# Four of 22 feed-forward input groups by Strassen's scheme, their weight differences formed by GpSimd

## The chip, the cores and the metric

The kernel runs on one core of a Trainium2 chip. The core has a matrix engine (TensorE, PE in the profile; its weight loads are shown apart as PEld), VectorE (DVE), ScalarE (ACT), GpSimd (POOL) and SyncE (SP), which here only issues DMAs. The metric is device time of one launch in microseconds, median of the runs.

## The reference

A decoder trunk on 256 tokens of width 2048, in float32. Layer 0 is a recurrent block, layer 1 is windowed attention with sinks, and each is followed by a feed-forward block of hidden width 5632. The feed-forward block is what the change touches:

```python
D_MODEL = 2048
SEQ = 256
D_FF = ((8 * D_MODEL // 3 + 255) // 256) * 256
...
def swiglu_ffn(x, g, w_in, w_out):
    h = rms_norm(x, g)
    gate, up = jnp.split(h @ w_in, 2, axis=-1)
    return x + (jax.nn.silu(gate) * up) @ w_out
...
for layer in range(DEPTH):
    ...
    x = swiglu_ffn(x, norm2_g[layer], ffn_w_in[layer], ffn_w_out[layer])
```

## The kernel before, in words

**Layout.** Activations are kept transposed: features on the 128 partitions, 256 tokens (T) along the columns, so x is 16 tiles of 128x256. Each float32 operand is split into a high part in the format fp32r and the rest, a low part of the same format; a product is three matmuls, high by high, high by low, low by high.

**Jobs.** All weight matrices are cut into jobs of 512 KB: 256 rows (two tiles of 128) by 512 columns, on the chip 128x1024. Every job goes the same way, in `stream` (L278): SyncE loads it into one of four `raw` buffers (`load`, four jobs ahead); ScalarE copies it to one of four `hi` buffers, which rounds it (L264), and VectorE subtracts, raw - hi, into one of four `lo` buffers (L267), three jobs ahead; then its matmuls run. A `hi` and `lo` pair comes free when TensorE has done the job four before; a `raw` buffer, when its split is done.

**Groups.** `group` (L347) runs the jobs of 512 output columns over the whole inner dimension, 8 jobs for an inner dimension of 2048: 4 column tiles by 2 row tiles by 3 products, 24 matmuls of 256 columns a job, weights loaded into the array and activations streaming. Sums stay in PSUM. Of four PSUM banks two are used whole ("two"): there the high weight may multiply the high and low part of the activations in one matmul of 512 columns. `products` (L296) puts three such matmuls in a row at set places (`SYNC`) and behind any other work of TensorE (`pe_other`, L334). A group with `paired` holds its four sums in two banks and has no 512-column matmuls.

**Feed-forward input.** 22 groups a layer. The columns of a group are gate, up, gate, up for two hidden tiles. At a group's end `done` brings the four sums from PSUM, scales them by the norm (`rstd`), and a background task does silu(gate) * up and splits it into a hidden tile. The norm's factor comes late, from `norm` (L466): TensorE sums the squares, and VectorE and ScalarE form the reciprocal root.

**Order.** The instructions are recorded job by job. Between them `run_bg` lets background tasks (evacuations, norms, gains, softmax) add instructions as long as estimates of VectorE's and ScalarE's time stay under limits. Each engine works its own queue in this order. Intermediate tiles are 58 numbered slots of 128x512 and 8 halves, reused first in, first out.

**GpSimd** does nothing before but the element-wise work of attention (L940, L942, L984).

## Time and profile before

| | |
|---|---|
| median of 3 runs | 1980.52 us (1980.26 to 1980.54) |
| profiled execution, first to last instruction | 1978.9 us |
| TensorE matmuls / weight loads busy | 1971.8 / 1930.5 us |
| VectorE / ScalarE / GpSimd busy | 1256.3 / 1063.0 / 70.5 us |
| HBM read | 371.88 MB, 189 GB/s over the span |
| granted TensorE clock | 1.00 in every stretch asked for |

In the groups of instructions a row gives line, engine, operation, output<-inputs by the program's names without their numbers, shape and count; then the busy time in us and the mean of one in ns; then the engine's idle time ahead of them and what ended it. In a timeline a row gives start, duration (of a row of equal instructions, from the first start to the last end), and in brackets the idle time just before. Records on one engine overlap a little, so the time that an instruction takes in a row is from start to start. A row of stretches gives for each engine the busy us and the number of instructions, then the clock, the share of the DMA engines and GB/s.

### The profile page before, as it was taken

Reading aid. Unit: us, or ns where it says so; the run is one execution under the profiler, and the core shown is the slowest. Engines: PE = TensorE matmul, PEld = TensorE weight load, DVE = VectorE, ACT = ScalarE, POOL = GpSimd, SP = SyncE. Lnnn points to the kernel's source line nnn. Section 1 sums busy time; section 2 is a strip of 40 time slices with the busy share of each in tenths; the row PEclk is TensorE's granted clock in tenths of the full one; section 3 lists DMA queues with packets and bytes.
Section 4 is the critical chain, followed back from the end, with each engine's and each line's share of the span. In section 5 each row is a group of like instructions: output and inputs, shape, how many; then the busy total and the mean of one; then the engine's idle time right before and its main releaser. Section 6 shows DMA issues by size and latency. Waiting matters only on the chain.

```text
span 1978.9 us, 40162 instructions
## 1 busy us (share of the span) xinstructions
PE 1971.8 (100%) x16683; PEld 1930.5 (98%) x16683; DVE 1256.3 (63%) x1981; ACT 1063.0 (54%) x1606; POOL 70.5 (4%) x100
## 2 busy tenths in 40 slices
PE   9999999999999999999999999999999999999999
PEld 9999999999999999999999889999999999999999
DVE  8988876556556655545668776755655565554443
ACT  7798655444444444434556775544544454443342
POOL 0000000000000000000002461000000000000000
PEclk9999999999999999999999999999999999999999
DMA  8555655655556555555655335555565556666663
GB/s 289 185 180 189 212 190 190 197 194 192 192 194 195 196 192 193 192 195 196 195 183 180 130 128 168 190 196 192 192 193 196 196 190 196 193 195 204 208 205 126
DMA packets 106198, 377.10 MB, mean 191 GB/s; under 512 B 11936, under 2 KB 14368, under 8 KB 106016
## 3 DMA queue, kind: packets, MB, share of 16 engines
q1 hardware_dynamic: 105408, 373.88, 57.7%
q8 instruction: 130, 2.13, 0.4%
q10 hardware_dynamic: 608, 0.66, 0.1%
q14 instruction: 52, 0.43, 0.1%
HBM read 371.88 MB, written 2.10 MB: 189 GB/s over the span
## 4 chain that ended last, share of the span: by engine, by line
PE 97%; ACT 1%; DVE 1%; issue 0%; POOL 0%; DMA 0%; ACTq 0%; POOLq 0%
PE b L330 93%; PE b L341 1%; PE b L664 1%; ACT s L116 1%; PE b L338 1%; PE b L850 1%; DVE lo L267 0%; ACT hi L264 0%; DVE s L918 0%; PE b L859 0%; PE b L860 0%; PE b L861 0%; DMA x<-in_x 0%; DVE s L125 0%; DVE s L129 0%
## 5 line engine op out<-in xcount | busy, mean ns | idle before, releaser
L330 PE MATMUL b<-s,hi 128*128 128x256 f32 (+1 forms) x10329 | 1432.1, 284 | 1.1 <-DVE h L125 0.6
L330 PEld LDWEIGHTS b<-s,hi 128*128 128x128 f32 x10329 | 1316.8, 188 | 30.5 <-ACT s L116 1.2
L267 DVE TENSOR_TENSOR lo<-raw,hi 128x1024 fp32r<-128x1024 f32 (+1 forms) x707 | 861.5, 1220 | 655.0 <-ACT hi L264 652.6
L264 ACT ACTIVATE hi<-raw 128x1024 fp32r<-128x1024 f32 (+1 forms) x707 | 746.1, 1056 | 808.6 <-PE b L330 750.7
L330 PE MATMUL b<-s,lo 128*128 128x256 f32 x5504 | 827.9, 276 | 0.0
L330 PEld LDWEIGHTS b<-s,lo 128*128 128x128 f32 x5504 | 718.3, 188 | 0.6
L940 POOL TENSOR_TENSOR s<-s 128x128 f32<-128x128 f32 x32 | 14.8, 463 | 1100.4 <-ACT s L116 1097.6
L116 ACT ACTIVATE s<-h 128x256 fp32r<-128x256 f32 (+1 forms) x106 | 40.7, 411 | 23.5 <-DVE h L125 23.5
L116 ACT ACTIVATE t<-b 128x256 f32<-128x256 f32 x130 | 47.9, 375 | 4.1 <-PE b L330 1.7
L116 ACT ACTIVATE s<-x,par 128x256 fp32r<-128x256 f32 x80 | 38.9, 499 | 20.4 <-DVE x L125 13.7
L116 ACT ACTIVATE s<-s 128x256 f32<-128x256 f32 (+2 forms) x116 | 41.7, 412 | 10.9 <-DVE s L129 7.5
L116 ACT ACTIVATE h<-h 128x256 f32<-128x256 f32 (+1 forms) x104 | 38.9, 376 | 3.7 <-DVE h L125 1.5
L116 ACT ACT_TABLE_LOAD x30 | 38.5, 1283 | 0.6
L129 DVE SCALAR_TENSOR_TENSOR s<-x,par,s 128x256 fp32r<-128x256 f32 x80 | 37.6, 479 | 1.8 <-ACT s L116 1.2
L125 DVE TENSOR_TENSOR x<-x,b 128x256 f32<-128x256 f32 x64 | 24.1, 415 | 21.2 <-PE b L330 21.2
L125 DVE TENSOR_TENSOR h<-b,rstd 128x256 f32<-128x256 f32 x100 | 37.5, 414 | 0.0
L125 DVE TENSOR_TENSOR h<-h,rstd 128x256 f32<-128x256 f32 x94 | 35.3, 416 | 0.0
L125 DVE TENSOR_TENSOR s<-s,s 128x256 fp32r<-128x256 f32 (+2 forms) x84 | 32.4, 416 | 4.1 <-ACT s L116 4.0
L125 DVE TENSOR_TENSOR h<-h,h 128x256 f32<-128x256 f32 x88 | 34.7, 415 | 0.5 <-ACT h L116 0.5
L125 DVE TENSOR_TENSOR s<-h,s 128x256 fp32r<-128x256 f32 x88 | 34.9, 417 | 0.1
L125 DVE TENSOR_TENSOR h<-b,t 128x256 f32<-128x256 f32 x92 | 34.5, 415 | 0.0
L116 ACT ACTIVATE s<-s,h 128x128 f32<-128x128 f32 x64 | 28.2, 442 | 10.2 <-DVE h L134 5.2
(99 smaller groups left out, 612.0 us busy)
## 6 DMA issues: line engine op xcount, KB each, us to landing
raw<-in_ffn_in SPq DMA_DIRECT2D x352, 512.0 KB, 3.4
raw<-in_ffn_out SPq DMA_DIRECT2D x176, 512.0 KB, 3.5
raw<-in_lru_in SPq DMA_DIRECT2D x62, 512.0 KB, 3.8
raw<-in_lru_out SPq DMA_DIRECT2D x32, 512.0 KB, 4.1
raw<-in_w_q SPq DMA_DIRECT2D x32, 512.0 KB, 3.4
raw<-in_w_o SPq DMA_DIRECT2D x32, 512.0 KB, 3.3
raw<-in_gate SPq DMA_DIRECT2D x8, 512.0 KB, 3.7
raw<-in_kv SPq DMA_DIRECT2D x8, 512.0 KB, 4.3
```

The source lines that it names most:

```text
L116: self.nc.scalar.activation(out, in_, func, **kw)
L125: self.nc.vector.tensor_tensor(out, a, b, op)
L129: self.nc.vector.scalar_tensor_tensor(out, a, s, b, op0, op1)
L264: high = self.ins(self.nc.scalar.activation(hi[:, q], raw[:, q], AF.Copy))
L267: self.nc.vector.tensor_tensor(lo[:, q], raw[:, q], hi[:, q].bitcast(F32), ALU.subtract)
L330: self.nc.tensor.matmul(*args, **kw)
L338: self.other = self.ins(f(*args, **kw))
L341: self.other = self.ins(f(*args, **kw))
L664: nc.tensor.matmul(out[j], (hi if high else lo)[:, c:c + P], x2[kt][:, q:q + T], start=kt == 0 and high > q, stop=kt == 1 and not high)
L850: nc.tensor.matmul(ps[f][:, 0:T], w0, x2[kt][:, q:q + T], start=k0 + kt == 0 and high > q, stop=k0 + kt == ND - 1 and not high)
L940: nc.gpsimd.tensor_tensor(o, o, sc[hh][:, 2 * P:3 * P], ALU.add)
```

## The change

In each layer's feed-forward input, groups 0 to 3 are done by Strassen's scheme (Winograd's form, with 7 products for 8). In a Strassen job the 256 rows are two row tiles, the tokens are two halves of 128, and the 512 columns are two halves of 256. So a 2x2 block of activations by a 2x2 block of weights takes 7 products, each three matmuls of 256 columns: 21 a job. Here activations are loaded into the array and the weights stream, and the result has tokens on the partitions.

- **Weights.** The host puts the job's four quarters in another order (`quarters`). Behind each load of such a job GpSimd forms the weight sums (`sums`): two in a slot (t), one in place in the raw buffer, one in a half (t4). `split` then makes high and low parts of raw (1024 columns), t (512) and t4 (256).
- **Activations.** For each pair of tiles `form` makes the four sums of activations: two scaled copies by ScalarE, four GpSimd instructions of 128x128, then a split. It is spawned by `residual` of the projection ahead, and waits for 14 free slots.
- **End of a group.** `fast` combines the four banks (ScalarE once, VectorE four times). Then come the norm's factor per token, silu and product; four transposes on TensorE bring the hidden tiles back to features on partitions. `norm` forms the factor per token too, now for each norm but the first (`if r`): two more sums of one column.
- **Order.** Four jobs of ordinary groups come first, then Strassen jobs and ordinary jobs in turns (32 of each), then the rest. Ordinary groups 4 to 8 have `paired` set to 2: two banks and no 512-column matmuls. The four-bank Strassen group and the two-bank ordinary one leave two banks for the rest.

The core of the diff, without the host's `quarters`, the calls in `run`, and the lines that only hand arguments on:

```diff
+    NS = 4
+    AHEAD = 4
+    SPACE = 14
...
+    def sums(self, i):
+        raw, tt = self.raw[i % 4], self.nc.gpsimd.tensor_tensor
+        b = [raw[:, q * T:(q + 1) * T] for q in range(4)]
+        t, t4 = self.slot(F32), self.half()
+        self.jobs[i][2].update(t=t, t4=t4)
+        t3, t2 = t[:, 0:T], t[:, T:2 * T]
+        tt(t3, b[2], b[0], ALU.subtract)
+        tt(b[0], b[0], b[1], ALU.subtract)
+        tt(t2, b[2], b[0], ALU.subtract)
+        tt(t4, b[3], t2, ALU.subtract)
+
     def split(self, i):
         raw, hi, lo = self.raw[i % 4], self.hi[i % 4], self.lo[i % 4]
+        if len(self.jobs[i]) > 2:
+            s = self.jobs[i][2]
+            t, t4 = s.pop("t"), s.pop("t4")
+            h, l, o = (self.slot() for _ in range(3))
+            s.update(h=h, l=l, o=o)
+            for z, a, b in ((raw, hi, lo), (t, h, l), (t4, o[:, 0:T], o[:, T:2 * T])):
+                self.nc.scalar.activation(a, z, AF.Copy)
+                self.nc.vector.tensor_tensor(b, z, a.bitcast(F32), ALU.subtract)
+            self.free(t)
+            self.free_half(t4)
+            self.dve += 1300
+            self.act += 1200
+            return
...
+    def strassen(self, src, xs, forms, done, last):
...
+                todo = [(0, 0, A(0, 0), B(1)), (1, 1, A(1, 0), B(3)), (1, 0, S(1), t2), (2, 0, S(0), B(0)),
+                        (2, 1, S(2), t3), (3, 0, S(3), B(2)), (3, 1, A(1, 1), t4)]
...
+                    for i, j in ((0, 0), (0, 1), (1, 0)):
+                        self.nc.tensor.matmul(ps[b][:, h * T:h * T + T], w[i], m[j], start=b not in st["begun"],
...
+    def form(self, c, col, out):
+        while len(self.slots) < self.SPACE:
+            yield 1
...
+        tt = self.nc.gpsimd.tensor_tensor
+        tt(s[0], a21, a22, ALU.add)
+        tt(s[2], a11, a21, ALU.subtract)
+        tt(s[1], s[0], a11, ALU.subtract)
+        tt(s[3], a12, s[1], ALU.subtract)
+        yield 3
+        fh, fl = self.slot(), self.slot()
+        self.a(fh, z)
+        self.tt(fl, z, fh.bitcast(F32), ALU.subtract)
...
-        if r == 2:
+        if r:
             n = T + 2
...
+            def fast(ps, g=g):
...
+                self.a(c1, ps[0][:, 0:T])
+                self.tt(two(U[:, :]), two(ps[1][:, :]), twice(c1[:, :]), ALU.add)
+                self.tt(two(V[:, :]), two(ps[2][:, :]), twice(U[:, 0:T]), ALU.add)
+                self.tt(U[:, 0:T], ps[2][:, 0:T], V[:, T:2 * T], ALU.add)
+                self.tt(V, ps[3], V, ALU.add)
...
+            turns += self.strassen(lambda c, g=g: w[g, c], xs, forms, fast, g == self.NS - 1)
+        for g in range(self.NS, NH // 2):
...
-            self.group(lambda c, g=g: w[g, c], ND, xs, done, g == NH // 2 - 1, self.SYNC)
+            self.group(lambda c, g=g: w[g, c], ND, xs, done, g == NH // 2 - 1, self.SYNC,
+                       paired=2 * (g <= 2 * self.NS), jobs=ordinary)
+        n = len(turns)
+        self.jobs += ordinary[:self.AHEAD]
+        for q in zip(turns, ordinary[self.AHEAD:]):
+            self.jobs += q
+        self.jobs += ordinary[self.AHEAD + n:]
```

How the queues change is seen in the order of instructions. VectorE in the first layer's feed-forward input before; lo, raw and hi are the split's buffers, h and s are halves and slots of the hidden tiles:

```order
L267 TENSOR_TENSOR lo_79<-raw_71,hi_75 128x1024
L125 TENSOR_TENSOR s_4346<-h_95,s_4346 128x256
L125 TENSOR_TENSOR s_4360<-h_97,s_4360 128x256
L267 TENSOR_TENSOR lo_80<-raw_72,hi_76 128x1024
L267 TENSOR_TENSOR lo_81<-raw_73,hi_77 128x1024
```

And in the changed kernel, in the turns; line 287 is the split of a Strassen job (raw, t, t4), line 299 that of an ordinary one:

```order
L299 TENSOR_TENSOR lo_82<-raw_74,hi_78 128x1024
L287 TENSOR_TENSOR lo_79<-raw_71,hi_75 128x1024
L287 TENSOR_TENSOR s_4659<-s_4629,s_4658 128x512
L287 TENSOR_TENSOR s_4660<-h_95,s_4660 128x256
L299 TENSOR_TENSOR lo_80<-raw_72,hi_76 128x1024
L287 TENSOR_TENSOR lo_81<-raw_73,hi_77 128x1024
```

Between two splits of 1024 columns there now stand one of 512 and one of 256, in every second job. GpSimd, whose queue is empty at this place before, has four instructions for each Strassen job (lines 273 to 276), two jobs shown:

```order
L273 TENSOR_TENSOR s_4090<-raw_73 128x256
L274 TENSOR_TENSOR raw_73<-raw_73 128x256
L275 TENSOR_TENSOR s_4090<-raw_73 128x256
L276 TENSOR_TENSOR h_100<-raw_73,s_4090 128x256
L273 TENSOR_TENSOR s_4157<-raw_71 128x256
L274 TENSOR_TENSOR raw_71<-raw_71 128x256
```

Each chain works on every second raw buffer. TensorE, at the change from an ordinary job (line 362, weights from hi and lo loaded) to a Strassen job (line 461, hi and lo streaming; names are streaming operand, then loaded one):

```order
L362 MATMUL b_88<-s_3827,hi_78 128x256 x2
L362 MATMUL b_88<-s_3827,lo_82 128x256
L461 MATMUL b_83<-hi_75,s_3470 128x256
L461 MATMUL b_83<-lo_79,s_3470 128x256
L461 MATMUL b_83<-hi_75,s_3470 128x256
L461 MATMUL b_90<-hi_75,s_3484 128x256
```

No 512-column matmul stands in the turns, where before there were three at each place of `SYNC`.

More of the change, by code (lines that the diff above doesn't have):

```diff
@@ new lines, in form @@
+    def form(self, c, col, out):
+        while len(self.slots) < self.SPACE:
+            yield 1
+        g, z = self.slot(F32), self.slot(F32)
+        for h in range(2):
+            k = 2 * c + h
+            self.a(g[:, h * T:h * T + T], self.x[k // 4][:, k % 4, :], scale=self.par[:, col + k:col + k + 1])
+        s = [z[:, n * P:n * P + P] for n in range(4)]
+        a11, a21, a12, a22 = (g[:, n * P:n * P + P] for n in range(4))
+        tt = self.nc.gpsimd.tensor_tensor
[7 more added lines that the diff above has]
+        self.tt(fl, z, fh.bitcast(F32), ALU.subtract)
+        self.free(g)
+        self.free(z)
+        out[c].ap = (fh, fl)
+        out[c].ready = True
+        yield
@@ L427, in gained @@
         xt = self.x[k // 4][:, k % 4, :]
-        for col, vals in gains:
+        for col, vals, *_ in gains:
             g = self.par[:, col + k:col + k + 1]
@@ L503, in residual, with form @@
             return
+        def form(c):
+            for q in gains:
+                if len(q) > 2:
+                    self.spawn(self.form(c, q[0], q[2]))
         def task():
@@ L1089, in run @@
         self.spawn(first())
-        self.lru([(C_N2A, x1)], 1)
-        self.ffn(0, x1, 1, [(C_KVG, xk)], 2)
+        f1, f3 = ([Val() for _ in range(ND // 2)] for _ in range(2))
+        self.lru([(C_N2A, x1, f1)], 1)
+        self.ffn(0, x1, f1, 1, [(C_KVG, xk)], 2)
         self.kv(xk, 2, [(C_N1B, x2)])
-        self.attn(x2, 2, [(C_N2B, x3)], 3)
-        self.ffn(1, x3, 3, None, None, out=d["out"])
+        self.attn(x2, 2, [(C_N2B, x3, f3)], 3)
+        self.ffn(1, x3, f3, 3, None, None, out=d["out"])
         self.stream()
```

89 lines of the change are left out of this document (86 added, 3 removed).

## Prediction

> **What bounds the kernel now.** I read the page's busy times and its chain first.
>
> ```profile
> PE   1971.8 (100%) x16683; PEld 1930.5 (98%) x16683; DVE 1256.3 (63%) x1981; ACT 1063.0 (54%) x1606; POOL 70.5 (4%) x100
> PE 97%; ACT 1%; DVE 1%; issue 0%; POOL 0%; DMA 0%; ACTq 0%; POOLq 0%
> ```
>
> TensorE is on the path for 97% of the span. So fewer matmuls should shorten it, as long as the engines that prepare its operands keep up. How far ahead they are is read from the timeline of a stretch in steady state.
>
> ```profile
> 900.03 1.06 ACT L264 ACTIVATE hi<-raw 128x1024 fp32r<-128x1024 f32 x1 [1.66 <-PE b L330]
> 901.13 1.23 DVE L267 TENSOR_TENSOR lo<-raw,hi 128x1024 fp32r<-128x1024 f32 x1 [1.48 <-ACT hi L264]
> 902.75 1.06 ACT L264 ACTIVATE hi<-raw 128x1024 fp32r<-128x1024 f32 x1 [1.66 <-PE b L330]
> 908.20 1.06 ACT L264 ACTIVATE hi<-raw 128x1024 fp32r<-128x1024 f32 x1 [1.67 <-PE b L330]
> ```
>
> The two engines split one job of weights at a time, and ScalarE starts each split when TensorE gives back a buffer. So the starts of its rows are TensorE's pace: 902.75 - 900.03 = 2.72 us for 24 matmuls of 256 columns, 0.1133 us each. The split that begins at 900.03 is done at 901.13 + 1.23 = 902.36, and its job starts on TensorE three jobs later, at 908.20. VectorE's lead is thus 5.8 us, and it idles 1.48 us a job.
>
> TensorE has a second, slower pace. Behind the sum for a norm (line 338) it stays there for a while:
>
> ```profile
> 306.58 0.59 PE L338 MATMUL b<-acc,con 128*128 128x256 f32 x2
> 307.24 1.10 PE L330 MATMUL b<-s,lo 128*128 128x256 f32 x8
> 326.67 1.23 DVE L267 TENSOR_TENSOR lo<-raw,hi 128x1024 fp32r<-128x1024 f32 x1 [1.60 <-ACT hi L264]
> 329.50 1.23 DVE L267 TENSOR_TENSOR lo<-raw,hi 128x1024 fp32r<-128x1024 f32 x1 [1.60 <-ACT hi L264]
> 900.74 1.07 PE L330 MATMUL b<-s,lo 128*128 128x256 f32 x8
> ```
>
> The same eight matmuls take 1.10 us at 307 and 1.07 us at 900, and a job 329.50 - 326.67 = 2.83 us: 0.118 us for a matmul, 0.0046 more.
>
> **The change, part by part.**
>
> *Matmuls removed.* A Strassen job has 21 matmuls of 256 columns where an ordinary one has 24. Two layers, 4 groups, 8 jobs, 3 each: 192 x 0.1133 = 21.8 us less TensorE work, 10.9 us a layer. The matmuls of 512 columns that vanish from the ordinary groups 4 to 8 are each replaced by two of 256. Those cost no time as such, but they are what the kernel puts behind a disturbance, and between the first and the last Strassen job there are none. So the slower pace can last there. I bound it by all and nothing of 1440 matmuls a layer: 0 to 6.6 us. The K/V projection, which also changes between jobs with weights and jobs with activations as the loaded operand, shows both paces by turns:
>
> ```profile
> 1029.30 0.39 PE L850 MATMUL b<-s,hi 128*128 128x256 f32 x2
> 1031.74 0.40 PE L850 MATMUL b<-s,hi 128*128 128x256 f32 x2
> ```
>
> I take half, 3.3 us a layer.
>
> *TensorE work added.* Four transposes a Strassen group, and two one-column sums (two passes each) in the norm.
>
> ```profile
> 1166.17 0.66 PE L341 MATMUL b<-con,s 128*128 128x128 f32 x4
> 1166.58 0.71 PE L330 MATMUL b<-s,hi 128*128 128x256 f32 x4
> 1025.73 0.50 PE L341 MATMUL b<-con,acc 128*128 128x1 f32 x4
> 1026.09 0.48 PE L850 MATMUL b<-s,hi 128*128 128x256 f32 x2
> ```
>
> From start to the next matmul's start: 0.41 us for four transposes, with the restart about 0.5; and 0.36 us for the columns. That is 4 x 0.5 + 0.4 = 2.4 us a layer. If TensorE stays the bound, a layer gains 10.9 - 3.3 - 2.4 = 5.2 us.
>
> *Work for GpSimd.* Each Strassen job has four TENSOR_TENSOR of 128x256, each operand from SBUF, with line 274 to 276 waiting on the one before. The trace has three groups on that engine:
>
> ```profile
> L942 POOL TENSOR_TENSOR s<-s,h 128x256 f32<-128x256 f32 x32 | 29.9, 955 | 0.2
> L984 POOL TENSOR_TENSOR s<-s,con 128x256 f32<-128x256 f32 x32 | 25.9, 811 | 28.6 <-ACT s L116 27.1
> L940 POOL TENSOR_TENSOR s<-s 128x128 f32<-128x128 f32 x32 | 14.8, 463 | 1100.4 <-ACT s L116 1097.6 <-PE b L341 2.7
> ```
>
> Those means hide two kinds of instruction, and the timelines of GpSimd and VectorE side by side tell them apart:
>
> ```profile
> 1085.12 0.53 DVE L918 CUSTOM_DVE_ANT_0 s<-b,con,par 128x256 f32<-128x256 f32 x1
> 1085.13 0.74 POOL L984 TENSOR_TENSOR s<-s,con 128x256 f32<-128x256 f32 x1
> 1089.66 1.19 POOL L942 TENSOR_TENSOR s<-s,h 128x256 f32<-128x256 f32 x2
> 1191.48 2.17 POOL L942 TENSOR_TENSOR s<-s,h 128x256 f32<-128x256 f32 x2
> 1191.91 1.26 DVE L267 TENSOR_TENSOR lo<-raw,hi 128x1024 fp32r<-128x1024 f32 x1 [0.57 <-ACT hi L264]
> 1193.61 2.42 POOL L984 TENSOR_TENSOR s<-s,con 128x256 f32<-128x256 f32 x2
> 1193.65 1.78 DVE L267 TENSOR_TENSOR lo<-raw,hi 128x1024 fp32r<-128x1024 f32 x1
> ```
>
> Beside a VectorE instruction with one operand in PSUM (line 918) GpSimd's takes 0.74 us and both run undisturbed. Beside a split (line 267, both operands in SBUF) one waits for the other: two of line 942 take 1.19 us at 1089.66 and 2.17 at 1191.48, around a split; and the split at 1193.65, behind a GpSimd instruction that began 0.04 us earlier, takes 1.78 instead of 1.23. So the two never read at once. A GpSimd instruction of 0.74 us takes 0.55 us from a VectorE instruction that waits for it; by the same 0.19 us less, the lighter line 942 (one operand a broadcast column) takes 0.60 - 0.19, about 0.4 to 0.47. The new instructions read two full operands like line 984, so I take 0.55, with 0.45 below and 0.74 above as ends.
>
> The Trainium skill states this as an exclusive lock on a port that VectorE and GpSimd share, held for the whole instruction (page "SBUF — State Buffer", section "SBUF: two separate sides"). That the two exclude each other the trace confirms; the whole instruction it doesn't, since 0.55 us were lost to one of 0.74. By the page's wording the price would be 0.74.
>
> *Work for VectorE.* Its time from start to start, in a row of instructions, is below the recorded mean:
>
> ```profile
> 37.43 3.49 DVE L267 TENSOR_TENSOR lo<-raw,hi 128x1024 fp32r<-128x1024 f32 x3
> 891.72 1.07 DVE L125 TENSOR_TENSOR x<-x,b 128x256 f32<-128x256 f32 x3
> L267 DVE TENSOR_TENSOR lo<-raw,hi 128x512 fp32r<-128x512 f32 x6 | 4.0, 691 | 3.8 <-ACT hi L264 3.7
> ```
>
> (3.49 - 1.23) / 2 = 1.13 us for 1024 columns, (1.07 - 0.41) / 2 = 0.33 for 256, and between them 0.60 for 512 (the row's 0.69 less the same overlap of 0.09). A Strassen job now needs a split of 1024, one of 512 and one of 256.
>
> *The sum on what the two engines share.* Per layer, from the split of the first Strassen job (job 4) to that of the last (job 66), these have both operands in SBUF, counted in the order of instructions: 63 splits of 1024 columns, 71.2 us; 32 of 512, 19.2; 32 of 256, 10.6; 29 others of 256 (products and splits of hidden tiles, the gains, the norm), 9.6; two of 512 for the last activation sums, 1.2. That is 111.8 us of VectorE. GpSimd adds 124 weight differences at 0.55 (those of the first Strassen job are done before), 68.2, and eight instructions of 128 columns at 0.46 - 0.19 = 0.27, 2.2. Together 182.2 us. VectorE has some 16 us more that read PSUM; these can run beside GpSimd, and I leave 2 us of them uncovered. So 184.2 us.
>
> TensorE starts job 4 three jobs after that first split may begin, 8.2 us, so it can start job 66 no earlier than 184.2 - 8.2 = 176.0 us after job 4. Before, those 62 jobs took 62 x 2.72 = 168.6. The lead is used up and TensorE then waits on VectorE: 7.4 us more a layer; its own added work disappears in these waits, except the last transposes and the slow pace until the next 512-column matmuls, less the shorter job 66, about 0.5. Two layers: 2 x 7.9 = 15.8 us. The profiled execution has 1978.9 us from first to last instruction, 1.6 under the median of 1980.52; I leave that as it is: 1980.5 + 15.8 = 1996.
>
> *Hidden elsewhere.* ScalarE gets 1.06 + 0.59 + 0.38 us for a Strassen job and 1.06 for an ordinary one, 3.1 us of the 5.4 of two jobs, so it isn't the bound. Loads take
>
> ```profile
> raw<-in_ffn_in SPq DMA_DIRECT2D x352, 512.0 KB, 3.4
> L116 ACT ACTIVATE s<-b 128x512 f32<-128x512 f32 x16 | 9.5, 594 | 7.5 <-PE b L341 7.4
> ```
>
> 3.4 us, and a raw buffer comes round every four jobs, 11 us. With four differences of up to 0.8 us each and a split of 2.4 us it is busy for 9 us: covered, but by 2 us only. Behind a load that waits for its buffer, SyncE's queue holds the next job's load, and ScalarE's queue holds the evacuations behind a split that waits for GpSimd. The activation sums of the earlier tiles are formed in the projection ahead, where GpSimd is idle; costed at nothing, since VectorE's spare 1.48 us a job covers their 0.60.
>
> **The rivals.**
>
> *TensorE stays the bound.* If handing over costs less than 0.47 us, because GpSimd's differences fall into VectorE's waits and its PSUM work, the shared time fits and the kernel gains 2 x 5.2 = 10.4 us: 1970, between 1964 (no slow pace) and 1977 (slow throughout). The attention stage is the nearest thing in the trace, by stretches of all instructions and of line 267 alone:
>
> ```profile
> 1100.00:1150.00 50.00, 50.00 (x428) 44.14 (x425) 35.16 (x119) 37.32 (x100) 27.03 (x38) 1.00 0.37 126
> 1100.00:1150.00 50.00, 14.24 (x12) 1.00 0.37 126
> ```
>
> For it: 38 GpSimd instructions in 50 us (the columns are TensorE, its weight loads, VectorE, ScalarE, GpSimd) go beside a TensorE that is busy throughout, and the change asks for 124 in 176, which is 35 in 50. Against: at the same prices those 38 cost (0.27 + 0.42 + 0.55) / 3 each, 15.7 us, and the 12 splits 13.6, so 29 of 50 us are taken there; the change asks for 182 of 169. Chance 0.26.
>
> *The two effects cancel.* A layer changes by 124 x (price - 0.486) us on this sum. At 0.47 to 0.50 us that is -2.0 to +1.7, or 1976 to 1984 for both. Chance 0.12.
>
> *The whole instruction is lost.* At 0.74 (and 0.46 for the short ones) the sum is 207.3 + 2 us, so 201.1 against 168.6: 33 us a layer, 2046. The same comes if VectorE's queue always goes first and the four dependent differences run only in its gaps; it decides from about 0.65 us (2021). For it: each of the four waits on the one before and can lose its turn four times. Against: at 1193 to 1196 us the engines took turns. Chance 0.10. By the page's sentence on the lock this would be the outcome; the 1.78 us row speaks for less.
>
> **How the numbers follow.** The forecast, VectorE and GpSimd together as the new bound at 0.50 to 0.65 us, has 0.52 and its own range 1984 to 2021; the likeliest is 1996. The whole range, leaving out about a tenth at each end, goes from 1967 to 2030. A measurement of this kernel tells a difference of 0.2%, 4 us, from none. Faster by more than that: the first rival and a little of the second, 0.28. Within it: 0.12. Slower: 0.60.
>
> **What would show it.** Right: in the stretch of the turns VectorE and GpSimd together are busy nearly all the time, splits (now at lines 287 and 299) often take 1.7 us or more, GpSimd's differences have a mean above 1 us, two jobs take 5.7 us or more instead of 5.44, and the waits of TensorE name VectorE's lo or the 512-column pieces. Wrong: TensorE has no idle time there and two jobs take 5.1 to 5.3 us (first rival); or splits of 2 us and more and a stretch of over 195 us (third). If instead TensorE waits for DMA or for PSUM banks at group ends, the raw buffers or banks were the limit and my sum was on the wrong resource.

## The result: 2081.06 us, 5% slower, and the profile after

The changed kernel takes 2081.06 us (median; 2079.94 to 2081.54) against 1980.48 of the kernel before, measured beside it: ratio 1.0504, 95% interval 1.0488 to 1.0521. A fourth run of the changed kernel took 3267.7 us at a granted clock of 0.56 and is left out of these numbers. The forecast was 1996 with a range up to 2030. The direction was right; the size, +100.6 us instead of +15.8, was not.

The page of the kernel after, busy times and the shares of the chain of work that ended last:

```profile
PE   2001.5 (96%) x16699; PEld 1956.2 (94%) x16699; DVE 1375.6 (66%) x2089; ACT 1126.6 (54%) x1754; POOL 368.5 (18%) x420
PE 75%; POOL 6%; DVE 6%; ACT 6%; issue 3%; DMA 3%; ACTq 0%; POOLq 0%; DVEq 0%; SPq 0%
```

TensorE had 97% of the chain; now GpSimd, VectorE and ScalarE have 6% each, in equal parts, and loads 3%. No engine has taken TensorE's place. The stretches of the turns say the same (busy us of TensorE, its weight loads, VectorE, ScalarE and GpSimd, then the clock):

```profile
350.00:400.00 50.00, 44.55 (x346) 43.63 (x346) 33.51 (x44) 23.82 (x37) 29.31 (x30) 0.90 0.50 157
400.00:450.00 50.00, 42.55 (x326) 40.95 (x325) 35.65 (x43) 23.23 (x35) 28.21 (x30) 0.90 0.50 159
```

In 50 us 346 and 326 matmuls are started, 7.7 and 7.2 pairs of jobs of 45: a pair takes 6.5 to 6.9 us. Yet VectorE is busy for 34 to 36 of 50 us and GpSimd for 29. Part of this is one held up by the other, so these times alone do not say whether the time that the two share is used up; e1 and e7 below do, which give them the same work in less time. Where every engine idles, something is done in sequence that could be done side by side. The groups of 310 to 500 us show who waits (mean ns of one, then idle time ahead and what ended it):

```profile
L287 DVE TENSOR_TENSOR lo<-raw,hi 128x1024 fp32r<-128x1024 f32 x28 | 41.6, 1485 | 0.3 <-ACT hi L286 0.3
L299 DVE TENSOR_TENSOR lo<-raw,hi 128x1024 fp32r<-128x1024 f32 x27 | 35.1, 1300 | 9.4 <-ACT hi L296 9.4
L274 POOL TENSOR_TENSOR raw<-raw 128x256 f32<-128x256 f32 x28 | 30.1, 1076 | 2.2
L273 POOL TENSOR_TENSOR s<-raw 128x256 f32<-128x256 f32 x28 | 29.8, 1064 | 70.8 <-DMA raw<-in_ffn_in 57.8 <-PE b L461 6.6 <-DVE s L129 3.3
L287 DVE TENSOR_TENSOR s<-s,s 128x512 fp32r<-128x512 f32 x27 | 20.1, 745 | 40.5 <-ACT s L286 40.5
L286 ACT ACTIVATE s<-s 128x512 fp32r<-128x512 f32 x28 | 17.7, 631 | 76.1 <-POOL s L275 76.0
```

ScalarE stands for 76 of 190 us ahead of the split of t, waiting for GpSimd's third difference; VectorE 40 us behind ScalarE; GpSimd 58 us for a load. Each of the three waits for another. The chain of work in order of time (start, length, what) shows the ring whole:

```profile
401.67 1.71 DVE lo L287
403.43 3.43 DMA raw<-in_ffn_in
...
407.00 0.86 POOL s L273
...
407.93 0.74 POOL raw L274
...
408.75 0.75 POOL s L275
...
409.57 0.77 POOL h L276
...
410.68 1.05 ACT hi L296
...
413.27 1.77 DVE lo L287
415.09 4.20 DMA raw<-in_ffn_in
```

VectorE's split frees a raw buffer (401.67); the next load goes into it (403.43); GpSimd makes four differences of it, one after another; ScalarE, which has waited for the last two, now makes the high part of the *ordinary* job (line 296) and then the raw split of its own job; VectorE follows, and the buffer is free again at 415.04. One round is 11.6 us from split to split, for the four jobs that TensorE does in 10.4. This round is a short one: at 6.5 to 6.9 us a pair, four jobs take 13.0 to 13.9 us. Why the ordinary job's split stands behind GpSimd's work is told by the order of instructions on ScalarE:

```order
L286 ACTIVATE s_4119<-s_4090 128x512
L286 ACTIVATE s_4121<-h_100 128x256
L296 ACTIVATE hi_76<-raw_72 128x1024
L286 ACTIVATE hi_77<-raw_73 128x1024
```

t and t4 of a Strassen job stand ahead of the split of the ordinary job that TensorE does first, and of their own job's raw split. VectorE's rows shown ahead of the prediction have the same order (s, s, then lo of the ordinary job, then lo of the Strassen job). They were recorded as raw, t, t4, behind the ordinary job. TensorE's waits over the whole run:

```profile
PE b L370 <- DVE s L133: 24.5, 7, 4.9
PE b L362 <- ACT hi L296: 17.2, 9, 4.4
PE b L461 <- ACT t L120: 13.6, 6, 2.7
PE b L461 <- DVE lo L287: 11.2, 13, 1.9
```

The first is not a split at all: transposes stand in TensorE's queue ahead of matmuls that could run, and wait for the products of line 133. The third is the evacuation of a Strassen group's banks, which also queues on ScalarE.

A measure used below is the time from the first matmul of a layer's first Strassen job to the first of its last. The prediction had 176.0 us for it. It came to 217.1 and 214.3.

### The profile page after: what moved, and what is told of

It reads as the page before. It is cut to its first block, busy times and chain, and to the rows that moved or that the text cites. A ratio compares the mean times of both kernels' runs of the same rounds, so it can differ in the third digit from the quotient of the medians.

```text
span 2078.8 us, 40908 instructions
## 1 busy us (share of the span) xinstructions
PE 2001.5 (96%) x16699; PEld 1956.2 (94%) x16699; DVE 1375.6 (66%) x2089; ACT 1126.6 (54%) x1754; POOL 368.5 (18%) x420
## 4 chain that ended last, share of the span: by engine, by line
PE 75%; POOL 6%; DVE 6%; ACT 6%; issue 3%; DMA 3%; ACTq 0%; POOLq 0%; DVEq 0%; SPq 0%
PE b L362 69%; DMA raw<-in_ffn_in 3%; PE b L461 3%; ACT hi L296 3%; ACT s L120 2%; DVE lo L287 2%; PE b L373 1%; DVE lo L299 1%; POOL s L273 1%; POOL h L276 1%; POOL s L275 1%; POOL raw L274 1%; DVE s L129 1%; PE b L370 1%; DVE h L129 1%
## 5 line engine op out<-in xcount | busy, mean ns | idle before, releaser
L362 PE MATMUL b<-s,hi 128*128 128x256 f32 (+1 forms) x9474 | 1316.9, 285 | 18.5 <-ACT hi L296 17.2
L362 PEld LDWEIGHTS b<-s,hi 128*128 128x128 f32 x9474 | 1214.4, 190 | 42.9 <-ACT hi L296 19.3
L299 DVE TENSOR_TENSOR lo<-raw,hi 128x1024 fp32r<-128x1024 f32 (+1 forms) x643 | 786.7, 1226 | 519.0 <-ACT hi L296 516.2
L362 PE MATMUL b<-s,lo 128*128 128x256 f32 x4992 | 753.5, 277 | 0.6 <-DVE lo L299 0.6
L461 PE MATMUL b<-hi,s 128*128 128x256 f32 x512 | 125.0, 285 | 15.3 <-ACT t L120 13.6
L461 PEld LDWEIGHTS b<-hi,s 128*128 128x128 f32 x512 | 93.8, 192 | 17.3 <-ACT t L120 14.8
L461 PE MATMUL b<-s,s 128*128 128x256 f32 x576 | 102.2, 287 | 0.0
L287 DVE TENSOR_TENSOR lo<-raw,hi 128x1024 fp32r<-128x1024 f32 x64 | 96.9, 1514 | 3.4 <-ACT hi L286 3.4
L461 PE MATMUL b<-lo,s 128*128 128x256 f32 x256 | 74.0, 289 | 11.2 <-DVE lo L287 11.2
L461 PEld LDWEIGHTS b<-s,s 128*128 128x128 f32 x576 | 84.2, 196 | 0.0
```

Of the source, the lines that this page charges most:

```text
L287: self.nc.vector.tensor_tensor(b, z, a.bitcast(F32), ALU.subtract)
L299: self.nc.vector.tensor_tensor(lo[:, q], raw[:, q], hi[:, q].bitcast(F32), ALU.subtract)
L362: self.nc.tensor.matmul(*args, **kw)
L461: self.nc.tensor.matmul(ps[b][:, h * T:h * T + T], w[i], m[j], start=b not in st["begun"], stop=c == ND // 2 - 1 and i == 1, skip_group_ch ...
```

## The experiments

Theory A: the exclusion of GpSimd and VectorE, inside a queue order that makes ScalarE and VectorE wait for GpSimd before they serve the job that is due first. Rivals: the ring through the raw buffer alone (too few buffers); the transposes; TensorE's own work; the length of the chain whatever its engines read.

**e1, the order mended.** Splits of t and t4 are forced behind the raw split of their own job, on both engines; nothing else.

```diff
-                self.nc.scalar.activation(a, z, AF.Copy)
-                self.nc.vector.tensor_tensor(b, z, a.bitcast(F32), ALU.subtract)
+                with ExitStack() as behind:
+                    if act is not None:
+                        behind.enter_context(self.tc.issue_after(act))
+                        behind.enter_context(self.tc.issue_after(dve))
+                    act = self.ins(self.nc.scalar.activation(a, z, AF.Copy))
+                    dve = self.ins(self.nc.vector.tensor_tensor(b, z, a.bitcast(F32), ALU.subtract))
```

> The split of a Strassen job is forced to stand in its own order on ScalarE and VectorE (raw, then t, then t4 of the same job), where the changed kernel has t and t4 of the next Strassen job ahead of the ordinary job's split. All else is kept. Theory loop (a raw buffer's round trip, load 4.3 us, four differences 4 to 5 us, then two splits queued on ScalarE behind them, 13.3 us for four jobs, sets the pace): the split of raw then needs only the second difference, the round trip falls under 10 us, and what is left is the predicted sum or TensorE: 1990 to 2030 us. Theory port (VectorE and GpSimd share one port and its sum is the pace): the work on the port is the same, 2070 to 2085. Theory TensorE queue (the transposes wait for VectorE in TensorE's queue and the clock falls behind each wait): 2060 to 2085.

Measured: 2030.55 us, ratio 1.0244 (1.0214 to 1.0273), 50.5 less than the change. From the first Strassen job to the last it is 196.1 and 191.2 us. The same two stretches as above:

```profile
350.00:400.00 50.00, 42.85 (x350) 42.15 (x350) 46.09 (x50) 26.99 (x42) 35.49 (x32) 0.93 0.52 169
400.00:450.00 50.00, 45.48 (x368) 45.28 (x367) 43.58 (x48) 26.31 (x42) 34.69 (x32) 0.93 0.50 169
```

VectorE's busy time goes from 34 to 36 us to 44 to 46. Half of the loss was order. The work that VectorE and GpSimd share is the same, so that work was not what took 2081 us; the time comes out just past the upper end of the figures for the loop.

**e2, six raw buffers,** filled six jobs ahead, with 55 slots instead of 58 and the order left to the scheduler.

```diff
-        raw, src = self.raw[i % 4], self.jobs[i][0]
+        raw, src = self.raw[i % 6], self.jobs[i][0]
```

> Six raw buffers instead of four, loads up to six jobs ahead (from job 33 on), three slots fewer to make room; the order on ScalarE and VectorE is as the scheduler makes it. Theory loop: a round trip of 13.3 us now serves six jobs, 4.4 us for two, so it is no longer the bound: 1990 to 2030 us. Theory port: 2070 to 2085. Theory TensorE queue: 2060 to 2085.

Measured: 2079.47 us, ratio 1.0491 (1.046 to 1.0521): nothing gained. Its waits from 300 to 520 us:

```profile
ACT s L286 <- POOL s L275: 66.3, 26, 4.9
POOL s L273 <- DMA raw<-in_ffn_in: 48.7, 20, 4.5
```

ScalarE waits for GpSimd much as before, though loads may start two jobs earlier. But the order is no longer that of the change. Three rows of ScalarE (others stand between them):

```profile
391.84 0.63 ACT L286 ACTIVATE s<-s 128x512 fp32r<-128x512 f32 x1 [3.45 <-POOL s L275]
...
393.94 1.05 ACT L286 ACTIVATE hi<-raw 128x1024 fp32r<-128x1024 f32 x1
...
401.14 1.04 ACT L286 ACTIVATE hi<-raw 128x1024 fp32r<-128x1024 f32 x1
```

The piece t made at 391.84 is of the job whose own raw split comes at 401.14; the raw split at 393.94 is of the Strassen job before it. The scheduler has put t and t4 one Strassen job further ahead: on ScalarE, t starts 9.8 us ahead of the raw split of its job (median of the first layer's 32), in the change 2.7. So the two buffers went into an order that waits for GpSimd still earlier. Whether the number of raw buffers sets the pace at the change's own order is not shown.

**e4, transposes later.** They are recorded eight half jobs later, order as in the change.

```diff
-                    yield 1
+                    yield 9
```

> The four transposes of a Strassen group are recorded eight half-ticks (four jobs) later, so that VectorE has made their inputs long before TensorE reaches them. Theory TensorE queue: the waits of TensorE for line 133, 24.5 us in all, go, and with them part of the stretches at half clock: 2030 to 2050 us. Theory loop and theory port: these waits only move to the next job's weights, 2065 to 2085.

Measured: 2071.84 us, ratio 1.0452 (1.0422 to 1.0482): 9 us less, though 24.5 us of waits had their name. TensorE's waits move to the splits:

```profile
PE b L362 <- ACT hi L296: 23.2, 21, 4.4
PE b L461 <- DVE lo L287: 20.5, 20, 2.4
```

**e5, fills in place of differences.** The Strassen products are then not those of the weights.

```diff
-        tt(t3, b[2], b[0], ALU.subtract)
-        tt(b[0], b[0], b[1], ALU.subtract)
-        tt(t2, b[2], b[0], ALU.subtract)
-        tt(t4, b[3], t2, ALU.subtract)
+        for o in (b[0], t3, t2, t4):
+            for _ in range(3):
+                self.nc.gpsimd.memset(o, 0.0)
```

> The weight differences are left out: GpSimd writes zeros to the same four places instead, three times each, so that it reads nothing, while raw, t and t4 still depend on a GpSimd chain behind the load (the products of the Strassen groups are then not those of the reference). If three memsets take about as long as one difference, the chain is as long as before but VectorE's splits of 1024 columns no longer wait for it (1.23 us instead of 1.5). Theory port: the shared time falls by its GpSimd part, 1970 to 1990 us. Theory loop: only the waits of the splits go, about 0.5 to 1 us of a round trip of 13.3: 2050 to 2075.

Measured: 1994.62 us, ratio 1.0070 (1.0047 to 1.0093), near the port's figure. I read this as the exclusion alone at first, and that was too quick. A fill reads nothing, so the scheduler put fills of t and t4 ahead of the load, and ScalarE's order changed with it. The experiment took away the chain and the exclusion together. e6 was made for that.

**e6, order mended, fills in a forced chain** behind the load, as long as four undisturbed differences.

```diff
+        prev = None
+        for o in (b[0], b[0], b[0], t3, t3, t2, t2, t4, t4):
+            with ExitStack() as behind:
+                if prev is not None:
+                    behind.enter_context(self.tc.issue_after(prev))
+                prev = self.ins(self.nc.gpsimd.memset(o, 0.0))
```

> The order of e1 on ScalarE and VectorE is kept. In place of the four differences GpSimd fills the same four places with zeros, nine fills of 0.313 us each, forced one behind the other, the first of them into the raw tile and so behind its load: 2.82 us from the load to the last of them, as long as four undisturbed differences (4 x 0.74 = 2.96), but GpSimd reads nothing. The Strassen products are then not the weights' (that part of the computation is left out). Theory A, exclusion: GpSimd and VectorE hold each other up, and this is what is left of the loss once the order is mended: splits of 128x1024 back at 1.23 us, time 1970 to 1990. Theory B, length of the chain load, GpSimd, ScalarE, VectorE, whoever reads what: time stays at 2020 to 2035.

Measured: 1976.48 us, ratio 0.9978 (0.9969 to 0.9988), turns of 166.7 and 165.5 us, and TensorE waits for nothing in them. A stretch of it:

```profile
400.00:450.00 50.00, 49.98 (x427) 49.64 (x425) 38.31 (x55) 29.93 (x46) 24.18 (x83) 1.00 0.57 197
```

And its ordinary splits from 310 to 470 us:

```profile
L306 DVE TENSOR_TENSOR lo<-raw,hi 128x1024 fp32r<-128x1024 f32 x32 | 39.1, 1221 | 4.3 <-ACT hi L303 4.2
```

Splits are back at 1.22 us beside a GpSimd that is busy half the time but reads nothing. A chain of 2.82 us through GpSimd costs nothing in this order. So what e1 has left over, 54 us, comes from the two engines reading SBUF. It also shows what the change is worth in this order of jobs without any wait of TensorE: a gain of 4.4 us.

**e10, the exclusion without a chain:** the kernel before, with the same 256 differences into a tile that nobody reads.

```diff
+        if i in self.extra:
+            tt(t[:, 0:T], b[2], b[0], ALU.subtract)
...
+        self.extra |= {len(self.jobs) + 4 + 2 * q for q in range(32)}
```

> The kernel before, with 64 times four differences of 128x256 by GpSimd that nobody waits for: written into a tile that nothing reads, at every second job of each feed-forward's first 64, behind that job's load. The result is unchanged. This is the exclusion without any chain behind it. VectorE's work of two ordinary jobs is 2 x (1.23 + 0.53) = 3.5 us. By the prediction's price, 0.55 us of VectorE's time lost for each difference, 3.5 + 2.2 = 5.7 us against TensorE's 5.44: 64 x 0.27 = 17 us more, about 1998, and VectorE busy or held up all the time. By the loss seen in e1's turns (splits of 128x1024 at 1.44 instead of 1.23 us, about 0.25 us lost for each difference) 4.5 us: TensorE stays the bound, 1979 to 1985, with splits of about 1.4 us.

Measured: 1981.12 us, ratio 1.0000 (0.9991 to 1.0009). A stretch of it:

```profile
350.00:400.00 50.00, 50.00 (x422) 49.14 (x422) 37.53 (x40) 24.26 (x31) 40.69 (x39) 1.00 0.60 204
```

Its splits, one of three groups of VectorE on hidden tiles, and one of its four differences, from 310 to 500 us:

```profile
L278 DVE TENSOR_TENSOR lo<-raw,hi 128x1024 fp32r<-128x1024 f32 x70 | 97.6, 1403 | 42.7 <-ACT hi L275 42.7
L127 DVE TENSOR_TENSOR s<-h,s 128x256 fp32r<-128x256 f32 x18 | 12.8, 748 | 0.2 <-ACT s L118 0.2
L257 POOL TENSOR_TENSOR scratch<-raw,scratch 128x256 f32<-128x256 f32 x29 | 31.6, 1090 | 2.3
```

The engines hold each other up here too (splits 1.40 instead of 1.22 us, the hidden tiles' instructions with both operands in SBUF 0.73 to 0.75 instead of 0.42, differences 1.00 to 1.17 instead of 0.74), but VectorE has the room and nobody waits for GpSimd. The prediction's price of 0.55 us for each difference, which gave 1998 here, is refuted as a fixed price: 70 splits lost 12.6 us and 54 instructions on hidden tiles 17.4 us to 117 differences, 0.26 each, and VectorE still had 42.7 us idle ahead of its splits.

**e7, e1 and late transposes.** The edits of e1 and e4 together.

> The order of e1, and the transposes recorded eight half jobs later (e4), so that they no longer stand in TensorE's queue ahead of the second products that they wait for: 15.4 us of such waits were left in one layer's turns of e1. If these waits are time of their own, about 10 to 15 us a layer less than e1: 2000 to 2015. Rival: as in e4 alone, where they went only -9 us and the wait moved to the splits, since VectorE (45 of 50 us busy in e1's turns) sets the pace anyway: 2020 to 2031.

Measured: 2015.18 us, ratio 1.0170 (1.0155 to 1.0185), turns of 187.5 and 185.9 us: 15.4 less than e1. The edit that gave 9 us in e4, where the waits moved to the splits, gives more here. A stretch of 50 us of its trace, and three of 5 us:

```profile
350.00:400.00 50.00, 46.92 (x376) 45.56 (x375) 47.21 (x52) 29.05 (x46) 37.39 (x32) 0.97 0.53 179
375.00:380.00 5.00, 4.73 (x41) 4.58 (x40) 5.00 (x6) 2.21 (x6) 4.62 (x5) 1.00 0.62 208
385.00:390.00 5.00, 4.23 (x37) 4.03 (x35) 5.00 (x8) 3.82 (x8) 3.64 (x5) 1.00 0.36 125
390.00:395.00 5.00, 3.62 (x19) 3.42 (x20) 5.00 (x6) 3.13 (x5) 3.00 (x4) 0.71 0.36 125
```

VectorE is busy or held up for all of each 5 us, and for 47.2 of the 50. Only here does the profile look as the prediction described it.

**e8, the differences by VectorE itself,** in the order of e1, and made ahead of their job's splits; GpSimd idles in the turns.

```diff
-        raw, tt = self.raw[i % 4], self.nc.gpsimd.tensor_tensor
+        raw, tt = self.raw[i % 4], self.nc.vector.tensor_tensor
```

> The order of e1, and the four differences made by VectorE itself, ahead of the splits of their job; GpSimd makes only the sums of the x tiles. No exclusion is left in the turns. In e6's turns VectorE was busy 38.2 of 50 us for 425 matmuls, 9.45 pairs of jobs, so 4.04 us a pair; the four differences add 4 x 0.416 (the 128x256 rows with both operands in SBUF of the kernel before) = 1.66: 5.70 us a pair against 5.28 of TensorE there. Theory A (VectorE's own sum sets the pace): 64 x 0.42 = 27 us over e6, about 2003, VectorE busy nearly all the time. If only the chain counted and VectorE's sum did not: like e1, 2030. If the exclusion cost less than 1.66 us of VectorE's time a pair, GpSimd's version e1 would be ahead of this one; by e1's 45.2 us for 364 matmuls, 5.6 us a pair, it is about even.

Measured: 1994.70 us, ratio 1.0067 (1.0054 to 1.0081), turns of 173.3 and 174.9 us; 36 us better than e1. Both of my figures were too pessimistic, and "about even with e1" was wrong.

```profile
400.00:450.00 50.00, 49.62 (x425) 49.41 (x423) 49.93 (x92) 30.74 (x47) 0.00 (x0) 1.00 0.58 192
```

VectorE is full, and TensorE nearly so in this stretch (46.58 of 50 us in the one before it). A difference handed to GpSimd costs more here than the same difference made by VectorE, 0.33 us from start to start by the prediction's row.

**Fewer turns.** e9 is e1 with one Strassen job to two ordinary ones, and with two banks for the ordinary groups up to number 12; e11 has late transposes as well, e12 is e11 with the differences by VectorE, and e13 is e11 with three groups and one Strassen job to three ordinary ones.

```diff
-        for q in zip(turns, ordinary[self.AHEAD:]):
-            self.jobs += q
+        for k, q in enumerate(turns):
+            self.jobs += [q] + ordinary[self.AHEAD + 2 * k:self.AHEAD + 2 * k + 2]
```

> The order of e1, and one Strassen job to two ordinary ones instead of one to one; the ordinary groups up to the thirteenth keep two banks. TensorE per turn 2.48 + 2 x 2.72 = 7.9 us; VectorE 4.6 + 1.8 us and 1.0 lost to GpSimd = 7.4. Theory A (what counts is VectorE's sum with the loss, per time): TensorE is the bound again, 1970 to 1990. Theory B (a chain of fixed length through every Strassen job's buffer, GpSimd, ScalarE and VectorE): the 64 chains cost what they cost in e1, 2015 to 2030.

> e9 (one Strassen job to two ordinary ones, GpSimd's differences) with the transposes eight half jobs later. A turn's VectorE work is e6's 4.04 + 1.76 for the second ordinary job + 1.5 lost to GpSimd = 7.3 us, TensorE's 7.9. In e9 9.8 us of TensorE's waits were for the second products. Theory A: with those gone little is left but TensorE's own work, 1980 to 1992. Rival: single differences held up still make single splits late (e9 waits for splits 3.7 us), and what e9 loses is not those waits: 1995 to 2003.

> As e11, but the differences by VectorE. VectorE's turn 4.04 + 1.76 + 1.66 = 7.5 us against TensorE's 7.9, and no exclusion. Theory A: TensorE is the bound, as in e6: 1976 to 1985, ahead of e11. Rival: VectorE works in order and waits at each Strassen job for its load, with ordinary splits queued behind: 1990 to 2005.

> e11 with three groups by Strassen's scheme instead of four, and one Strassen job to three ordinary ones. 144 matmuls of 0.1133 us are saved, 16.3 us, of the 192 and 21.8 us. VectorE's turn 4.04 + 2 x 1.76 + 1.5 = 9.1 us against TensorE's 10.6. e6 kept 4.4 us of 21.8; by the same share 3.3 us of 16.3 here. Theory A: TensorE is the bound, 1976 to 1981. Rival: single late splits remain, 1983 to 1992.

Measured: 2002.47 us (1.0110, 1.0095 to 1.0126), 1987.16 (1.0031, 1.0019 to 1.0043), 1988.36 (1.0036, 1.0024 to 1.0049) and 1985.84 (1.0026, 1.0016 to 1.0036). e9 lies between its two figures, e11 where theory A had it, e12 above its own. With room on VectorE the loss shrinks, so its sum does count, and who makes the differences no longer matters. But e13 missed 1976 to 1981. Its rival's figure, 1983 to 1992, was hit by luck: TensorE waits for no split in its turns. Its page has

```profile
PE   1976.8 (100%) x16811; PEld 1945.1 (98%) x16811; DVE 1345.8 (68%) x2041; ACT 1107.2 (56%) x1704; POOL 324.6 (16%) x356
```

TensorE is busy throughout, with 144 matmuls saved, and longer than before (1971.8). In its trace 5273 steps from one 256-column matmul to the next have the slow pace (0.115 to 0.13 us) against 1303 before; 3970 x 0.0047 = 18.7 us, more than the 16.3 saved.

**e15 and e16, disturbances kept out of the turns:** transposes wait until the last Strassen job is done, and two whole ordinary groups with 512-column matmuls stand between the norm and the first turn; e15 on e13, e16 on e6.

```diff
-    AHEAD = 4
+    AHEAD = 16
...
+                    while not over:
+                        yield 1
```

> e13 (three groups, one Strassen job to three ordinary ones, GpSimd's differences) with two edits that keep disturbances out of the turns: the transposes of all Strassen groups wait until the last of them is done, and two ordinary groups with their 512-column matmuls stand between the norm and the first turn instead of half a one. In e13 TensorE waits for nothing in the turns, and yet 1985.8 us came out; its trace has 5273 matmuls of 256 columns at the slow pace of 0.118 us, the kernel before 1303. Theory S (the slow pace is what remains): some 3300 fewer of them, 0.0047 us each, 15 us: 1968 to 1975, ahead of the kernel before. Rival: the pace follows from the order of accumulation into half banks, not from what precedes: the count stays above 4000 and the time at 1982 to 1988.

> e6 (zeros filled in a forced chain in place of the differences, so that the Strassen products are not the weights' and nothing is shared with VectorE; four groups, turns one to one) with the same two edits as e15. This is the change's own TensorE work without its waits and without the slow pace. e6 has 3463 slow matmuls against 1303 before. Theory S: 2000 fewer, 9 to 10 us less than e6: 1965 to 1969. Rival: pace follows from the half banks: 1974 to 1979.

Measured: 1987.46 us (1.0030, 1.0018 to 1.0041) and 1973.65 (0.9964, 0.9952 to 0.9977), with 5239 and 3425 slow steps. e15 is its rival's figure; e16 gains 2.8 us on e6 where theory S asked for 9 to 10, just past its rival's range, and its count hardly moves. The slow pace needs no transposes and no norm. In e15's timeline, ahead of the first turn and behind it:

```profile
331.40 1.07 PE L367 MATMUL b<-s,lo 128*128 128x256 f32 x8
...
335.94 0.28 PE L466 MATMUL b<-hi,s 128*128 128x256 f32 x1
...
340.30 1.10 PE L367 MATMUL b<-s,lo 128*128 128x256 f32 x8
```

Eight ordinary matmuls take 1.07 us before one Strassen job (line 466) and 1.10 after it.

**e17 and e18, which part starts the pace.** e17 is the kernel before with groups 4 to 8 in two banks and no more; e18 is e15 with a Strassen job's matmuls in another order.

```diff
+                       paired=2 * (4 <= g <= 8))
...
-                for n, (b, h, w, m) in enumerate(todo):
-                    for i, j in ((0, 0), (0, 1), (1, 0)):
+                for n, (b, h, w, m) in enumerate(todo + todo):
+                    for i, j in ((0, 0), (0, 1)) if n < 7 else ((1, 0),):
```

> One part of the change alone: the kernel before, with the five ordinary groups 4 to 8 of each feed-forward accumulated in two banks, two half banks each, as the change has them, and so without 512-column matmuls. No Strassen job, no difference. 5 x 8 x 24 x 2 = 1920 matmuls. If the half banks themselves bring the slow pace: 1920 more of the 0.118 us kind than the 1303 before, 1920 x 0.0047 = 9.0 us, 1988 to 1991. If a slow pace has to be started by something else (fp32 work, a Strassen job) and only lasts there: the pace of the group ahead goes on, 1980 to 1983.

> e15 with the 21 matmuls of a Strassen job in another order: first the two of each of the seven products that share a stationary tile (the rounded form by the rounded weights and by their remainder), then the seven with the form's remainder, as ordinary jobs order theirs. In e15 the slow pace begins at the first Strassen job's second matmul, behind 64 fast ones, with no fp32 work near. If that order of stationary tiles starts it: slow matmuls from 5239 down to under 2500, 13 us less, 1970 to 1976, ahead of the kernel before. If it is the half banks, or the roles of the operands, nothing changes: 1984 to 1989.

Measured: 1980.49 us (0.9996, 0.9987 to 1.0005) with 1293 slow steps, and 1989.63 (1.0035, 1.0023 to 1.0048) with 5434. Half banks in ordinary jobs do not bring the pace, and this order of products does not remove it. A Strassen job starts it: in both layers of e15 the steps are 0.113 us up to its second matmul and 0.118 behind that. The two-bank jobs carry it on; that they do so for want of 512-column matmuls is argued, as no run put any into the turns. What in a Strassen job starts it stays open: its operands have changed roles, and no run took that apart. No version made the right result faster than the kernel before.

## Why the prediction went wrong, step by step

One order of undoing accounts for 100.2 of the 100.6 us: the order of the splits 50.5 (e1), transposes in TensorE's queue 15.4 (e7), GpSimd and VectorE holding each other up 38.7 (e6 against e7), and TensorE's own work, a gain of 4.4. In another order the parts are other sizes: e4 alone is worth 9, since waits hide behind each other. The kernel before itself lay between 1980.5 and 1982.0 us from series to series, so each part is good to one or two us.

- **TensorE was the bound, VectorE's lead 5.8 us:** right, and not enough. The lead is three jobs deep, but the queue holds it in order; it is used up as soon as one instruction at its head waits.
- **"Hidden elsewhere" is the step that failed.** The text saw that "ScalarE's queue holds the evacuations behind a split that waits for GpSimd", found the ring through the raw buffer covered "by 2 us only", and costed both at nothing. It added each engine's time and assumed that the queues would let them overlap. The instruction order printed ahead of it already had t and t4 ahead of the ordinary job's split. With that order a pair takes 6.5 to 6.9 us, and from the first Strassen split of a layer to the last VectorE idles for 58 of 216 and 59 of 214 us. e1 shows that the order made it: with the same four raw buffers and the same work the stretch shrinks to 197 and 190 us. e2 does not settle what more buffers alone would do.
- **The shared sum:** the mechanism was right and the sum good to 3%, but the lead that was taken off it was too large. The sum gave 184.2 us from the split of the first Strassen job to that of the last. Once order and transposes are out (e7), this stretch takes 189.8 and 185.9 us; first e7, then the same stretches of e6, where GpSimd reads nothing:

```profile
299.54:489.31 189.77, 177.33 (x1436) 172.54 (x1435) 178.60 (x195) 107.84 (x169) 149.94 (x131) 0.98 0.50 170
1284.88:1470.73 185.85, 172.04 (x1415) 168.13 (x1414) 180.03 (x193) 105.65 (x162) 142.86 (x128) 0.99 0.52 174
296.07:463.77 167.70, 167.60 (x1425) 166.52 (x1425) 133.82 (x195) 108.07 (x171) 87.78 (x287) 1.00 0.58 198
1258.85:1424.62 165.77, 165.77 (x1419) 165.72 (x1418) 132.01 (x193) 108.14 (x169) 87.92 (x286) 1.00 0.58 200
```

From it the prediction took 8.2 us, three jobs of lead, and got 176.0 for TensorE's turns. In e7 TensorE starts its first Strassen job 4.3 and 1.9 us after the split of that job begins, and the last job's first matmul comes 2.0 us after the last split; the turns are 187.5 and 185.9 us. That is 11 us a layer, 2017 for both, against 2015 measured. For the same number of instructions VectorE is busy 44.8 and 48.0 us longer in e7 than in e6: 0.36 to 0.39 us lost for each of 124 differences. The 0.55 counted shared time, part of which was to lie beside VectorE's work from PSUM, so this does not contradict it; but e10 pays 0.26 and no time at all. The 0.55 came from a split that arrived second; who arrives second depends on who is queued.
- The Trainium skill (page "SBUF — State Buffer", section "SBUF: two separate sides") has the lock held for the whole instruction, and only against a GpSimd operation that reads SBUF. That fills do not disturb splits agrees (e6, 1.22 us). With 0.74 us for each difference the sum was 209.3 us a layer; e7's stretches of 189.8 and 185.9 speak for less.
- **Transposes** were costed as TensorE's work, 0.5 us a group. Their cost was their place: queued one background step behind the products that they wait for, and TensorE's queue held runnable matmuls behind them.
- **Slow pace:** half of 6.6 us a layer was taken. e6 counts 2160 more slow steps than before, 10.2 us for both layers instead of 6.6, and of the 21.8 us saved all else (transposes, columns, the step from one kind of matmul to another) took 21.8 - 10.2 - 4.4 = 7.2 instead of 4.8. So the first rival, TensorE as the bound at 1970, would have been 1976.5.
- **What would show it:** Two jobs above 5.7 us held. GpSimd's differences had a mean of 1.06 and 1.09 us for the first two of a job but 0.88 and 0.91 for the others, 0.98 in all, just short of the 1 us named. "Together busy nearly all the time" held in form, since one of the two was busy for 200 of the 216 us between the first layer's first and last Strassen split; but VectorE itself idled for 58, so the sign did not tell the forecast from what happened. TensorE's largest waits did not name lo. The text's own sign of a wrong resource, waits for banks at group ends, was there with 13.6 us. The third rival asked for a stretch over 195 us with splits of 2 us; the stretch came, with splits of 1.3 to 1.5. It was long for another reason.
- **What is not settled:** how 54 us (e1 against e6) divide between VectorE's lost time and single splits that come late; e11 to e13 only show that room on VectorE removes nearly all of it.

## What to carry to other kernels

When a helper engine is put ahead of in-order queues, read the new instruction order for each engine and ask of each instruction that waits for the helper what stands behind it; adding up busy times bounds the kernel only if that answer is "nothing that is due earlier". Elementwise work moved from VectorE to GpSimd is no help when both read SBUF: here VectorE lost 0.36 to 0.39 us to each difference that GpSimd made (e7 against e6), and makes one itself in 0.33; where VectorE had room it made no difference (e11, e12). And a scheme that saves one matmul in eight has to keep the habits that made the other seven quick: here the pace alone took back 10 of 22 us.

## What the runs showed of the hardware, unexpected

- **The clock falls after short waits.** In e7's turns TensorE waits for 1.6 us at the longest, yet the granted clock is 0.71 in the stretch from 390 to 395 us shown above, behind steps of 1.05 us (from 388.88) and 1.66 us (from 390.61) from one matmul to the next. The Trainium skill (page "TensorE: Matmul & The Clock Gate", Part 1) ties half rate to an idle window of about 3.4 us; here a window that was idle in part was enough. In the clock's records of the change and of e1, e2, e4, e5, e7, e8 and e9, 51 half-rate stretches follow full clock. In each run they begin on a grid of 3.41 us, each behind a step of it in which no matmul is recorded for 47% of the time or more; none of the other 4607 steps at full clock has more than 50%. Two waits in e7 about as long as those two, at 483.4 and 485.6 us, were not followed by a fall: a boundary of the grid, at 484.3, divides them. In the changed kernel 209 steps from one 256-column matmul to the next last 0.21 to 0.22 us, in e6 27: 182 x 0.1, so by estimate some 18 us more of TensorE's time is clock. How much of that lengthened the kernel is not shown.
- **The exclusion costs the pair, not one side.** In e10 splits lost 0.18 us each, VectorE's instructions on hidden tiles 0.31 to 0.33 and differences some 0.26 to 0.43, and the kernel lost nothing.
- **A run of three 512-column matmuls does not always end the slow pace.** In the trace of before, 20 such runs out of 32 that began in the slow pace were followed by it still.
